# Gate of the RWKV/Fourier mixer: ScalarE copies the product out of PSUM, then one tanh and one VectorE product

## The chip, the cores and the metric

One core of one Trainium2 chip runs the whole program in one launch. The metric is the device time in microseconds (us). The engines that this text names are PE (TensorE, the matrix products), DVE (VectorE), ACT (ScalarE), POOL (GpSimd) and SP (SyncE, which issues most DMAs). Each engine works off its own row of instructions; semaphores between the engines make an instruction wait until its operands are there and its destination is free.

## The reference, cut to what matters

Two blocks follow each other, each with two layers. The change lies in the even layer of the second block, whose mixer is

```
u = h @ w_in
s, gate_r, four, gate_f = jnp.split(u, ...)
s = s + (shift_fn(s) - s) * mu          # r, k0, v and the small inner layers
... the RWKV recurrence in two directions gives o, then a norm over each head ...
yr = o * jax.nn.silu(gate_r)
yf = fourier_mix(four) * jax.nn.silu(gate_f)
return jnp.concatenate([yr, yf], axis=-1) @ w_out
```

`silu(g)` is `g * sigmoid(g)`, and the kernel forms twice that as `(tanh(g / 2) + 1) * g`; the factor of two is put into other constants. `gate_r` has six tiles of 128 channels and `gate_f` two, so there are eight such gates. A tile has 768 columns: 256 of the context (`TC`) and 512 of the grid (`T`), together `CT`.

## The kernel before

Every product of the projection is made in three matrix products of split fp32 (high times high, low times high, high times low). `project_in` computes one tile of `h @ w_in`: 24 matmuls of 256 columns into the PSUM tile `ipc` and 24 of 512 columns into the PSUM tile `ipm`. Both have one buffer each, so the next projection can't begin in `ipc` before the last reader of the previous `ipc` is done.

What reads them depends on the projection. For `v`, `r` and `k0` it is `shifted`: ACT copies both tiles into the SBUF tile `u` (one buffer), scales it into `out`, and six DVE instructions add the shifted parts from `u`. For a gate it is `project_gate`, the function that the change edits: two tanh of ACT read PSUM, and two DVE products read PSUM once more. The results of all of them (`v`, `r`, `k0`, `sg`) stand in seven rotating SBUF buffers with the tag `rkv` (`NRKV = 7`), except for one Fourier gate, which has its own place.

The channels go in six pairs of heads, p = 0 to 5. `slot(i)` for i = 0 to 11 works off the recurrence of pair i // 2 in direction i % 2 (a chain of small matmuls `ch` and DVE instructions `zd`), and prepares the next one: products `gb`, an inverse by back substitution on DVE (`un`, `tmp`), which goes out and back through DRAM (`ad`, `blocks`), and `couple` (the matmuls `p`, then `pb`). Beside it runs the side work: in even slots `keys` (the norm `hst`, `hr`, `rt`, then the broadcast matmuls `hbc` and `hbm`, then `kk`) and `prepare` (`wlc`, `wl`, `alm`, then `sig`, `kd`, three scans into `L`, then `DC`, `F` and `L` on ACT); in odd slots `prepare` alone and `bonus` (`o`, `boc`, `bom`). The projections fill PE between these steps, in the order

```
for p in range(6):
    if p < 5:
        tasks += [self.project_pair(hs, P[p + 1], p + 1, n) for n in ("v", "r")]
    tasks += [self.project_gate(hs, P[p], p)]
    if p < 4:
        tasks += [self.project_pair(hs, P[p + 2], p + 2, "k0")]
```

Below, v4 is the projection of `v` for pair 4, g2 the gate of pair 2, and so on. The code gives the order of the work; a scheduler then settles the order in each engine's row by its own estimate of when each instruction could run, so that an edit in one function can move instructions of others.

Of the kernel before, what the change touches and what calls it, by code (L numbers as in the profile page):

```python
# [10 lines left out]
AF = mybir.ActivationFunctionType  # L11
ALU = mybir.AluOpType
# [5 lines left out]
TC = 256  # L18
# [130 lines left out]
class K:  # L149
# [1197 lines left out]
    def project_gate(self, hs, S, p, key="sg", **place):  # L1347

        pc, pm = yield from self.project_in(hs, 20 + p)
        sg = self.e("sg", [self.CT], **(place or dict(tag="rkv", bufs=self.NRKV)))  # L1350
        self.act(sg[:, :TC], pc, AF.Tanh, scale=0.5)
        self.act(sg[:, TC:], pm, AF.Tanh, scale=0.5)
        self.stt(sg[:, :TC], sg[:, :TC], 1.0, pc, ALU.add, ALU.mult)
        self.stt(sg[:, TC:], sg[:, TC:], 1.0, pm, ALU.add, ALU.mult)
        S[key] = sg

    def prepare(self, S, p, d):
# [679 lines left out]
```

## Time and profile before

| what | value |
|---|---|
| time, three runs | 3367.13, 3380.83 and 3379.16 us, median 3379.16 |
| the profiled execution's own time | 3377.71 us |
| its span, first to last instruction | 3376.0 us |
| mean granted clock of PE | 0.962 of full speed |
| PE busy | 3165.4 us (94% of the span) |
| DVE busy | 1834.4 us (54%) |
| ACT busy | 1189.2 us (35%) |
| slots 0 to 11 with what stands between them | about 2200 to 2960 us of the span |

The shares are means over the whole program. The part in which the gates stand is less than a quarter of the span. Times below are counted from the span's start.

### The profile page before, as it was taken

What the parts mean: (1) busy time and instruction counts of PE and PEld (TensorE: products, weight loads), DVE (VectorE), ACT (ScalarE), POOL (GpSimd) and SP (SyncE); (2) the same over time, 40 slices, a digit from 0 to 9 for tenths busy, and PEclk for the clock granted to TensorE, in tenths of its full rate; (3) what the DMA queues carried; (4) which work ended last, traced back from release to release, by engine and by line L of the source; (5) the groups of instructions that cost most, each with busy time, mean ns of one, the idle gap of its engine ahead of it and who ended that gap; (6) DMA issues with size and microseconds to landing.
All of it is one profiled execution on the core that took longest, in us unless ns stands there. A gap on an engine that the chain in (4) does not pass through costs nothing. (4 is left out here: it accounts for less than half of the span.)

```text
span 3376.0 us, 58396 instructions
## 1 busy us (share of the span) xinstructions
PE 3165.4 (94%) x24530; PEld 2646.8 (78%) x24530; DVE 1834.4 (54%) x3336; ACT 1189.2 (35%) x1925; POOL 287.1 (9%) x285
## 2 busy tenths in 40 slices
PE   5999999999999999999999979999898899869998
PEld 4877887888889888878887868788787778758766
DVE  8554378444425554364667456456655655462554
ACT  4222244432223222344322234233332432242553
POOL 3000020200002000111000010011101111020000
PEclk8999999999999999999999989999999999979999
DMA  6555421144433554332355521211110111222112
GB/s 238 191 181 178 134 82 44 51 145 143 131 96 120 185 176 164 121 102 78 117 182 182 163 87 46 72 31 38 32 30 22 29 58 30 59 67 63 62 39 69
DMA packets 156503, 340.90 MB, mean 101 GB/s; under 512 B 52816, under 2 KB 64848, under 8 KB 156112
## 3 DMA queue, kind: packets, MB, share of 16 engines
q1 hardware_dynamic: 156240, 337.18, 30.8%
q8 instruction: 192, 3.15, 0.4%
q14 instruction: 71, 0.58, 0.1%
HBM read 328.20 MB, written 8.91 MB: 100 GB/s over the span
## 5 line engine op out<-in xcount | busy, mean ns | idle before, releaser
L169 ACT ACTIVATE whi<-raw 128x1024 fp32r<-128x1024 f32 (+2 forms) x451 | 426.0, 947 | 1122.1 <-PE po L174 266.4
L253 DVE TENSOR_TENSOR wlo<-raw,whi 128x1024 fp32r<-128x1024 f32 (+2 forms) x432 | 471.3, 1093 | 539.7 <-ACT whi L169 528.8
L313 DVE CUSTOM_DVE_ANT_0 raw_a<-raw_a,cond 128x1024 f32<-128x1024 f32 x176 | 215.4, 1230 | 339.2 <-DMA raw_a<-in_ada_w_dram 339.1
L174 PE MATMUL pu<-hh,whi 128*128 128x512 f32 (+1 forms) x824 | 317.5, 385 | 5.0 <-ACT whi L169 5.0
L174 PE MATMUL pu<-hh,wlo 128*128 128x512 f32 (+1 forms) x824 | 316.5, 384 | 2.9 <-DVE wlo L253 2.9
L174 PE MATMUL pu<-hl,whi 128*128 128x512 f32 (+1 forms) x824 | 316.2, 384 | 0.0
L174 PE MATMUL pg<-hh,whi 128*128 128x512 f32 (+1 forms) x752 | 293.6, 391 | 22.1 <-ACT hh L169 20.0
L174 PE MATMUL po<-ah,whi 128*128 128x512 f32 (+1 forms) x880 | 309.7, 352 | 3.0 <-ACT sq L169 3.0
L174 PE MATMUL po<-ah,wlo 128*128 128x512 f32 (+1 forms) x880 | 308.7, 351 | 0.0
L174 PE MATMUL po<-al,whi 128*128 128x512 f32 (+1 forms) x880 | 308.0, 350 | 0.0
L174 PE MATMUL pg<-hl,whi 128*128 128x512 f32 (+1 forms) x752 | 291.9, 389 | 5.2 <-DVE hl L188 5.2
L174 PE MATMUL pg<-hh,wlo 128*128 128x512 f32 (+1 forms) x752 | 292.3, 389 | 4.4 <-DVE wlo L253 4.2
L402 POOL TENSOR_TENSOR x<-x,y 128x256 f32<-128x256 f32 x106 | 77.2, 763 | 2107.7 <-DVE y L188 2107.4
L174 PEld LDWEIGHTS pg<-hh,whi 128*128 128x128 f32 x752 | 147.1, 196 | 53.7 <-ACT hh L169 22.2
L174 PEld LDWEIGHTS pu<-hh,whi 128*128 128x128 f32 x824 | 159.0, 193 | 37.4 <-ACT whi L169 5.8
L174 PEld LDWEIGHTS po<-ah,whi 128*128 128x128 f32 x880 | 166.2, 189 | 27.5 <-ACT sq L169 3.8
L174 PEld LDWEIGHTS pu<-hh,wlo 128*128 128x128 f32 x824 | 158.2, 192 | 36.1 <-DVE wlo L253 4.5
L174 PEld LDWEIGHTS po<-al,whi 128*128 128x128 f32 x880 | 166.2, 189 | 23.5
L174 PEld LDWEIGHTS po<-ah,wlo 128*128 128x128 f32 x880 | 166.2, 189 | 23.3
L174 PEld LDWEIGHTS pu<-hl,whi 128*128 128x128 f32 x824 | 158.6, 193 | 31.9
L174 PEld LDWEIGHTS pg<-hh,wlo 128*128 128x128 f32 x752 | 146.3, 195 | 37.5 <-DVE wlo L253 8.4
L174 PEld LDWEIGHTS pg<-hl,whi 128*128 128x128 f32 x752 | 146.0, 194 | 36.0 <-DVE hl L188 6.7
(468 smaller groups left out, 6507.5 us busy)
## 6 DMA issues: line engine op xcount, KB each, us to landing
raw<-in_w_dram SPq DMA_DIRECT2D x232, 512.0 KB, 4.1
raw_a<-in_ada_w_dram SPq DMA_DIRECT2D x176, 512.0 KB, 3.7
raw<-in_ev_in_dram SPq DMA_DIRECT2D x60, 256.0 KB, 2.6
raw<-in_w_dram SPq DMA_DIRECT2D x32, 384.0 KB, 3.6
raw_a<-in_ada_w_dram SPq DMA_DIRECT2D x32, 256.0 KB, 5.6
raw<-in_ab_in_dram SPq DMA_DIRECT2D x16, 512.0 KB, 3.2
raw<-in_ev_out_dram SPq DMA_DIRECT2D x20, 256.0 KB, 2.7
raw<-in_w_dram SPq DMA_DIRECT2D x16, 256.0 KB, 2.6
```

The source lines that it names most:

```text
L169: ins = self.nc.scalar.activation(out=out, in_=in_, func=func, scale=scale, bias=bias)
L174: self.last_mm = self.nc.tensor.matmul(out, lhsT=lhsT, rhs=rhs, start=start, stop=stop)
L253: (self.nc.gpsimd if self.nwt <= self.POOLW else self.nc.vector).tensor_tensor(out=lo, in0=src, in1=hi.bitcast(F32), op=ALU.subtract)
L313: self.nc.vector.tensor_tensor_reduce(out=out, in0=raw, in1=v, scale=1.0, scalar=0.0, op0=ALU.mult, op1=ALU.add, accum_out=dst[:, o : o + 1])
L402: done = (self.nc.vector if last and k % 2 == 0 and (c0 or k > 4) else self.nc.gpsimd).tensor_tensor(out=new, in0=new, in1=y[k - 1][:, col ...
```

## The change

`project_gate` gets a tile `u`, which is the buffer that `shifted` uses too (same name, same shape, one buffer). ACT copies `ipc` and `ipm` into it; one tanh of 768 columns and one DVE product of 768 columns read the copy.

```
         pc, pm = yield from self.project_in(hs, 20 + p)
         sg = self.e("sg", [self.CT], **(place or dict(tag="rkv", bufs=self.NRKV)))
-        self.act(sg[:, :TC], pc, AF.Tanh, scale=0.5)
-        self.act(sg[:, TC:], pm, AF.Tanh, scale=0.5)
-        self.stt(sg[:, :TC], sg[:, :TC], 1.0, pc, ALU.add, ALU.mult)
-        self.stt(sg[:, TC:], sg[:, TC:], 1.0, pm, ALU.add, ALU.mult)
+        u = self.e("u", [self.CT])
+        self.act(u[:, :TC], pc, AF.Copy)
+        self.act(u[:, TC:], pm, AF.Copy)
+        self.act(sg, u, AF.Tanh, scale=0.5)
+        self.stt(sg, sg, 1.0, u, ALU.add, ALU.mult)
         S[key] = sg
```

The rows of the engines change in more places than these. ACT's row in slot 4, from the second tanh of `sig` on (`hr` is the inverse norm, `rt` its copy for the broadcast, `u` the copied projection, `whi` the high part of a weight), before:

```order
L169 ACTIVATE kd<-alm,a0h 128x512
L169 ACTIVATE whi<-raw 128x512
L169 ACTIVATE u<-ipm 128x512
L169 ACT_TABLE_LOAD
L169 ACTIVATE hr<-hst 128x12
L169 ACT_TABLE_LOAD
L169 ACTIVATE DC<-L 128x12
L169 ACTIVATE F<-L 128x12x64
L169 ACTIVATE r<-u,omu 128x768
L169 ACTIVATE rt<-hr 128x768
L169 ACTIVATE L<-L 128x768
```

and after:

```order
L169 ACTIVATE kd<-alm,a0h 128x512
L169 ACTIVATE whi<-raw 128x512
L169 ACTIVATE DC<-L 128x12
L169 ACTIVATE F<-L 128x12x64
L169 ACT_TABLE_LOAD
L169 ACTIVATE hr<-hst 128x12
L169 ACT_TABLE_LOAD
L169 ACTIVATE L<-L 128x768
L169 ACTIVATE rt<-hr 128x768
L169 ACTIVATE u<-ipc 128x256
L169 ACTIVATE whi<-raw 128x512
L169 ACTIVATE u<-ipm 128x512
```

`DC` and `F`, which read the scans, now stand ahead of `hr` and `rt`, and the copies of g3 stand behind `rt`; the projection r4, whose copies stood here, has moved to the slot before. In slot 2 the row has the same turn, and there it is the copy `u<-ipm` of v3 that stands behind `DC`, `F`, `hr` and `L`. Slot 6 is as slot 4.

PE's row in slot 4, around the broadcast `hbc` and `hbm` of the norm and the first matmuls `p` of `couple` (`ipc` and `ipm` are a projection's two PSUM tiles), before:

```order
L174 MATMUL hbc<-cst,rt 128x128 x2
L174 MATMUL hbm<-cst,rt 128x128 x4
L174 MATMUL ipm<-ehh_14770,wlo 128x512
L174 MATMUL ipm<-ehh_14772,whi 128x512
L174 MATMUL ipm<-ehl_14773,whi 128x512
L174 MATMUL ipm<-ehh_14772,wlo 128x512
L174 MATMUL ipm<-ehh_14774,whi 128x512
L174 MATMUL ipm<-ehl_14775,whi 128x512
L174 MATMUL ipm<-ehh_14774,wlo 128x512
L174 MATMUL p_20410<-tn,am_20402 64x64 x16
```

and after:

```order
L174 MATMUL ipm<-ehl_14775,whi 128x512
L174 MATMUL ipm<-ehh_14774,wlo 128x512
L174 MATMUL hbc<-cst,rt 128x128 x2
L174 MATMUL hbm<-cst,rt 128x128 x4
L174 MATMUL ipc<-ehh_14760,whi 128x256
L174 MATMUL ipc<-ehl_14761,whi 128x256
L174 MATMUL ipc<-ehh_14760,wlo 128x256
L174 MATMUL ipc<-ehh_14762,whi 128x256
L174 MATMUL ipc<-ehl_14763,whi 128x256
L174 MATMUL ipc<-ehh_14762,wlo 128x256
```

Before, the rest of g3 (7 matmuls) stands between the broadcast and `p`. Now g3 is complete ahead of the broadcast, and k5 begins behind it: 22 matmuls of 256 and 12 of 512 columns stand ahead of `p`, and the other 2 and 12 behind its first group.

ACT's row in slot 3, around the gate g2, before:

```order
L169 ACTIVATE DC<-L 128x12
L169 ACTIVATE F<-L 128x12x64
L169 ACTIVATE kd<-kd,oka,kah 128x768
L169 ACTIVATE L<-L 128x768
L169 ACTIVATE sg<-ipc 128x256
L169 ACTIVATE sg<-ipm 128x512
L169 ACTIVATE whi<-raw 128x512
L169 ACTIVATE u<-ipc 128x256
```

and after:

```order
L169 ACTIVATE DC<-L 128x12
L169 ACTIVATE F<-L 128x12x64
L169 ACTIVATE kd<-kd,oka,kah 128x768
L169 ACTIVATE L<-L 128x768
L169 ACTIVATE whi<-raw 128x512
L169 ACTIVATE sg<-u 128x768
L169 ACTIVATE u<-ipc 128x256
L169 ACTIVATE u<-ipm 128x512
```

The tanh of g2 keeps its place; its copies have gone to slot 2, and right behind it stand the copies of k4 into the same buffer `u`. On DVE the product `sg<-sg,u` stands where the two products stood, behind `kd<-kd,k`, `kk` and `o<-kd`. In slot 4 and in slot 6 DVE's three scans `L<-ec,sig`, which stood within the back substitution, now stand behind all of it but its last step, and the six instructions of r4 (r5 in slot 6), which stood behind it, within it. In slot 7, PE's row has no projection left ahead of `p`: the matmuls `eoc` and `eom` of the output projection stand there instead.

## Rows read from the trace of the kernel before

**Rows 1.** What PE waited for, 2200 to 2960 us: total, times, longest.

```profile
PE ipc L174 <- DVE sg L188: 32.2, 4, 10.4
...
PE p L174 <- DVE tn L1538: 4.3, 2, 2.2
```

**Rows 2.** PE in slot 3: start, duration, instruction, idle time before and its releaser.

```profile
2419.10 0.59 PE L174 MATMUL alm<-al,a2t 64*128 64x512 f32 x1
2430.11 0.58 PE L174 MATMUL ipc<-ehh,whi 128*128 128x256 f32 x1 [10.42 <-DVE sg L188]
2430.48 0.41 PE L174 MATMUL ipc<-ehl,whi 128*128 128x256 f32 x1
2430.70 0.42 PE L174 MATMUL ipc<-ehh,wlo 128*128 128x256 f32 x1
```

**Rows 3.** ACT in slot 3.

```profile
2428.36 0.38 ACT L169 ACTIVATE sg<-ipc 128x256 f32<-128x256 f32 x1 [0.44 <-DVE kd L183]
```

**Rows 4.** DVE in slot 3.

```profile
2427.38 0.95 DVE L183 TENSOR_TENSOR kd<-kd,k 128x768 f32<-128x768 f32 x1
```

**Rows 5.** All instructions with tile sg: shortest, median, longest in ns.

```profile
L169 ACT ACTIVATE sg<-ipc x8: 383/383/386, 2117.5 to 2711.1; 128x256 f32<-128x256 f32 x8
L188 DVE SCALAR_TENSOR_TENSOR sg<-sg,ipc x8: 405/410/423, 2117.9 to 2711.5; 128x256 f32<-128x256 f32 x8
L169 ACT ACTIVATE sg<-ipm x8: 574/586/592, 2122.0 to 2711.9; 128x512 f32<-128x512 f32 x8
L188 DVE SCALAR_TENSOR_TENSOR sg<-sg,ipm x8: 675/678/684, 2123.2 to 2712.7; 128x512 f32<-128x512 f32 x8
L188 DVE SCALAR_TENSOR_TENSOR o<-o,lb,sg x6: 1018/1019/1019, 2357.7 to 2944.5; 128x768 f32<-128x768 f32 x6
```

**Rows 6.** ACT in slot 2.

```profile
2365.97 0.58 ACT L169 ACTIVATE u<-ipm 128x512 f32<-128x512 f32 x1
2366.57 1.28 ACT L169 ACT_TABLE_LOAD   x1
...
2369.49 0.83 ACT L169 ACTIVATE F<-L 128x768 f32<-128x768 f32 x1
...
2372.52 0.62 ACT L169 ACTIVATE whi<-raw 128x512 fp32r<-128x512 f32 x1
```

**Rows 7.** DVE in slot 2.

```profile
2365.07 1.86 DVE L1388 TENSOR_TENSOR_SCAN L<-ec,sig 128x256 f32<-128x256 f32 x3 [0.59 <-ACT sig L169]
```

**Rows 8.** PE in slot 2.

```profile
2366.64 0.28 PE L174 MATMUL ipc<-ehh,whi 128*128 128x256 f32 x1
2366.76 0.28 PE L174 MATMUL ipc<-ehl,whi 128*128 128x256 f32 x1
2366.89 0.40 PE L174 MATMUL ipm<-ehh,whi 128*128 128x512 f32 x1
2367.12 0.40 PE L174 MATMUL ipm<-ehl,whi 128*128 128x512 f32 x1
```

**Rows 9.** DVE in slot 4.

```profile
2506.11 0.17 DVE L183 TENSOR_TENSOR un<-un,tmp 96x26 f32<-96x26 f32 x1
...
2509.66 2.78 DVE L188 SCALAR_TENSOR_TENSOR r<-u,mug,r 128x504 f32<-128x504 f32 x5 [2.64 <-ACT r L169]
```

**Rows 10.** PE in slot 4.

```profile
2510.45 0.67 PE L174 MATMUL hbc<-cst,rt 128*128 128x128 f32 x4
...
2515.80 1.67 PE L174 MATMUL p<-tn,am 64*64 64x64 f32 x48 [2.16 <-DVE tn L1538]
2518.42 3.00 PE L174 MATMUL p<-g,blocks 64*64 64x64 f32 x48 [0.95 <-ACT g L169]
```

**Rows 11.** DVE in slot 7.

```profile
2702.71 1.04 DVE L1538 STREAM_TRANSPOSE tn<-blocks 128x512 f32<-128x512 f32 x2 [3.22 <-DMA blocks<-ad]
```

**Rows 12.** PE in slot 7.

```profile
2705.47 1.61 PE L174 MATMUL p<-tn,am 64*64 64x64 f32 x48
...
2719.74 0.33 PE L174 MATMUL pb<-gb,tn 64*64 64x64 f32 x4 [0.33 <-DVE tn L183]
```

## The prediction

> **What bounds the kernel now.** I read the list of what PE waited for first, because PE is busy 94% of the span and a change elsewhere counts only through it. Between 2200 and 2960 us one entry is far above the rest: the first matmul of a projection (`ipc`) waits 32.2 us in four waits for a DVE instruction on `sg`, the longest 10.4 [rows 1]. So a gate's late reading of PSUM does stop PE. The timeline of PE shows where: in slot 3, `alm` is issued at 2419.10 and the next matmul only at 2430.11, after 10.42 us [rows 2]. Slots 5 and 7 repeat it.
>
> Why is the gate late there? ACT's row has the tanh of `sg` at 2428.36, released by `kd` of DVE [rows 3]: the tanh writes an `rkv` buffer, and the last reader of its former content is `kd<-kd,k`, at 2427.38 for 0.95 us [rows 4]. The gate therefore waits for a slot in SBUF, and holds its two PSUM tiles meanwhile. A copy into another tile doesn't need that slot. That is the good side of the change. The cost of the stall goes beyond the idle time: behind it 256-column matmuls start 0.22 us apart (2430.48 to 2430.70 [rows 2]) and in an undisturbed stretch 0.12 (2366.64 to 2366.76 [rows 8]), the lower of the two clock levels against the higher. About 20 matmuls run so, some 20 x 0.10 = 2.0 us.
>
> **The edit by itself.** For one gate ACT loses tanh of 0.38 and 0.59 us and gets two copies of the same shapes and source, taken as equal, and a tanh of 768 columns, 0.83 by the nearest row, `F<-L` [rows 5, 6]: 8 x 0.83 = 6.6 us more on an engine that is busy 35%. DVE loses 0.41 + 0.68 = 1.09 and gets one product of 768 columns, no dearer than `o<-o,lb,sg` at 1.02 and taken as 0.95 like `kd<-kd,k` [rows 5, 4]: 8 x 0.14 = 1.1 us less. Either sum is hidden where PE has work queued, and counts in full only where a wait hangs on it: from -1.1 to +6.6 us.
>
> The Trainium skill, "VectorE: DVE Perf Modes", Rules for kernel authors, advises to copy out of PSUM first only where many operations follow. Here one follows, and the rows agree that little is saved on DVE (0.14 us a gate); by that rule alone the sum would be the 6.6 us of ACT at worst.
>
> **What moves.** The order of the rows decides more than these sums, slot by slot. Two things matter: `u` is one buffer shared with `shifted`, and ACT's row is worked off in order.
>
> *Slot 2.* Before, ACT copies `ipm` of v3 at 2365.97 for 0.58 us, and r3 writes `ipm` at 2366.89 without a wait [rows 6, 8]. Now the copy stands behind `DC`, `F`, `hr` with two table loads, `L` and `whi`. The scans end at 2365.07 + 1.86 = 2366.93 [rows 7]; then 0.2 + 0.83 + 1.28 + 0.2 + 1.28 + 0.83 + 0.62 + 0.58 (durations of rows 6, the small ones and `L` as `F`) gives 2372.7, so 5.8 us of new idle time on PE. The 2.9 us of k4 that this slot takes over (12 x 0.12 + 7 x 0.23 less what slack there is) partly fill waits of `couple`. From +5.8 to +9; I take +7.
>
> *Slot 3.* v4 can't begin before k4 has been copied to `u`, and that copy waits for the gate's product. The first DVE product ended as PE was released, at 2430.1. In its place stands one of 0.95, then a copy of 0.38: 2430.1 - 0.41 + 0.95 + 0.38 = 2431.0 [rows 2, 4, 5]. So the wait stays, ending 0.9 later; k4's 16 matmuls (3.2 us) now run before it, and 23 instead of 37 stand behind it. I take -0.8, between +0.9 and -2.4.
>
> *Slot 4.* Before, `hbc` starts at 2510.45 and `p` at 2515.80, after 2.16 us of idle time [rows 10]. Now six `shifted` instructions (2.78 for five [rows 9]) stand in the back substitution and the scans behind it; the two swaps about cancel, so the last but one step of `un` ends near 2506.2 [rows 9]. Then scans 1.86, `DC` and `F` 1.0, load, `hr`, load 2.8, `L` and `rt` 1.65 (as in slot 2): `hbc` at 2513.5. g3 has been used up by then and k5 needs `ipc`, copied behind `rt`; PE idles some 5 us. Behind `hbc` (1.4 us with `hbm`) 22 x 0.12 + 12 x 0.23 = 5.4 us of k5 stand before `p`: 2520.3, so +4.5 at the higher clock. The 14 matmuls behind the first group of `p` (3.0 us) cover its 0.95 us wait: +2.0. If the clock has fallen, up to 34 x 0.10 = 3.4 more: I take 1. Sum +7.5, from +4 (the cover is better) to +10.
>
> *Slot 5.* About 4.4 us of work (12 matmuls of 256, 13 of 512 columns) have gone to slot 4. The wait of 10.4 us stays and ends 0.9 later, as in slot 3; what is missing stood between the groups of `couple`, where waits for ACT and DVE remain. Between 0 and -4.4, I take -1.7.
>
> *Slot 6.* As slot 4, with g4 and g5, and with the split of the Fourier part (`eyl`) in DVE's row ahead of `up`. +9, from +5 to +11.
>
> *Slot 7.* No projection is left to wait for PSUM. `p` can start when the blocks are back, 2702.71 + 1.04 = 2703.75, or at 2702.7 with its first half, against 2705.47 [rows 11, 12]: -2.5. From `p` to `pb` it took 14.25 us [rows 12]; without the last 11 matmuls of g5 (2.5 us) -2.5. Sum -5.
>
> *Slot 10* has a few matmuls between other groups: +1, between 0 and +2. The other slots keep their order up to a few rows: 0. The extra time on ACT is within these terms.
>
> **Sum.** 7 - 0.8 + 7.5 - 1.7 + 9 - 5 + 1 = +17.0 us on 3377.7 (span 3376.0 and 1.7 around it): 3394.7. The median of the runs is 1.5 higher than the profiled execution: 3396. Adding all lower bounds and all upper bounds gives +3 and +33; single terms being independent, I take 3384 to 3411 for this case.
>
> **Rivals.**
> *A, the stalls go.* The copies free PSUM early, as the code reads, and the three waits of 10.4 us vanish with their slow matmuls: 3 x (10.4 + 2.0) = 37 us, 3341. For it: four waits of PE on `sg` carry 32.2 us [rows 1]. Against: `p` can't come earlier than the blocks (in slot 7, 2.8 us [rows 11, 12]), so more likely 10 to 25 us: 3353 to 3368. It decides if the copies of g2 and g3 let k4 and k5 finish before the stall and nothing new is late in slots 2, 4 and 6, as where the scans come early enough to hide the turn of ACT's row.
>
> The Trainium skill, "Perfetto Trace Analysis", Optimization Strategy, reads gaps that repeat as too few buffers for the next tile; by that rule freeing PSUM early would take these three away, 37 us. The trace agrees that a buffer is what is missing, but of SBUF, and `u` would be the next one.
>
> *B, nothing on balance.* The stall moves from PSUM to `u`, and the turned rows of slots 2, 4 and 6 find slack: new waits of about 2 us each instead of 5, as `p` waited for the blocks anyway (4.3 us in two waits [rows 1]). 3 x 2 - 5 = +1: 3370 to 3384.
>
> *C, worse.* The clock falls behind each new wait and stays low for a whole `couple` (some 10 us of PE at half speed, 5 us each): 3396 + 3 x 5 = 3411 and more.
>
> **How the numbers follow.** Forecast 0.60 (0.38 of it above 3396), B 0.22, A 0.14, C 0.04. No change within 0.5%, about what a measurement of this kernel can tell, is 3362 to 3396: 0.22 and 0.22 less the part of A that lies there, some 0.44 in all; slower 0.38 + 0.04 = 0.42; faster 0.14. The range reaches from 3360, which cuts most of A, to 3412, which cuts C.
>
> **What would show it.** Right: in slots 2, 4 and 6 PE has new waits of 5 to 7 us ended by ACT (`u` or `rt`); in slots 3 and 5 a wait of 8 and 11 us remains, ended by ACT `u` and no longer by DVE `sg`; in slot 7 `p` starts about 2.5 us sooner after the blocks' issue. Each step is wrong if these rows are absent: if `u` ends no long wait in slots 3 and 5, A holds; if `p` in slots 4 and 6 still waits for `tn`, the inverse and not the broadcast is last there, and B holds. What would upset the sum most is the scans: if they come earlier than reckoned, the terms of slots 2, 4 and 6 (+23.5) shrink together.

## The result and the profile after

| | before | after |
|---|---|---|
| median of five runs of each, one chip | 3379.08 us | 3396.86 us |
| lowest to highest | 3367.13 to 3380.83 | 3395.53 to 3404.26 |
| ratio after / before, 95% interval | | 1.0066 [1.0048, 1.0084] |
| profiled execution, its span | 3377.7, 3376.0 | 3404.26, 3402.5 |

The change costs 17.8 us by the medians. The profiled execution of after is the slowest of its five, 7.4 us above their median, so what follows, read from it, adds up to more than that. First the page of after, span and busy times:

```profile
span 3402.5 us, 58400 instructions
...
PE 3178.3 (93%) x24530; PEld 2648.1 (78%) x24530; DVE 1834.8 (54%) x3328; ACT 1198.1 (35%) x1933; POOL 293.8 (9%) x285
```

The spans differ by 26.5 us, and nothing on this page says why: the same matmuls, and DVE and ACT as far from full as before. What PE waited for between 2200 and 2990 us (total, times, longest) is the view that answers to [rows 1]; it reaches 30 us further, since the slots end later. One more entry of before stands below it:

```profile
PE ipc L174 <- ACT u L169: 23.1, 4, 11.4
PE hbc L174 <- ACT rt L169: 14.8, 5, 4.8
PE eoc L174 <- ACT u L169: 11.4, 1, 11.4
PE eoc L174 <- ACT eyh L169: 5.3, 2, 4.3
PE ipc L174 <- ACT whi L169: 4.4, 1, 4.4
PE p L174 <- DVE tn L1539: 3.1, 1, 3.1
```

```profile
PE hbc L174 <- ACT rt L169: 5.7, 3, 2.9
```

The reader is to see two things. The long waits on the gate haven't gone, they have changed hands: `sg` of DVE ended 32.2 us of them [rows 1], and `u` of ACT now ends 23.1 + 11.4 us. And there are new ones: one on `whi`, and two long ones on `rt`, which ended three short waits before. Both are instructions of ACT.

The span can be laid out by slots. Each `couple` has one first `pb` on PE; a slot is here the stretch from the first `pb` of the couple before it to its own. The starts (us), from PE's timeline of each kernel, the first being that of the main couple ahead of slot 0, the second that of slot 0:

```
before 2179.67 2250.89 2322.33 2391.99 2459.02 2526.09 2592.63 2659.68 2719.74 2791.11 2852.09 2911.51
after  2182.76 2256.53 2327.84 2405.56 2475.53 2548.93 2612.81 2688.28 2741.40 2812.20 2874.05 2937.43
```

Slot 2, say, took 2391.99 - 2322.33 = 69.66 us and takes 2405.56 - 2327.84 = 77.72. In the same way for all slots, and for the experiments below, each against before (us, one profiled execution each):

| kernel | ahead of slot 0 | 0 | 1 | 2 | 3 | 4 | 5 | 6 | 7 | 8 | 9 | 10 | slots 0 to 10 |
|---|---|---|---|---|---|---|---|---|---|---|---|---|---|
| after | 3.1 | 2.6 | -0.1 | 8.1 | 2.9 | 6.3 | -2.7 | 8.4 | -6.9 | -0.6 | 0.9 | 4.0 | +22.8 |
| old_order | 0.2 | 2.7 | 0.0 | 0.0 | -2.5 | -0.7 | -1.0 | -0.9 | -1.8 | -1.5 | 0.8 | 0.0 | -4.9 |
| turned_back | 6.8 | 1.2 | -0.2 | 7.6 | 3.1 | 1.8 | -2.1 | 5.3 | -6.8 | -1.1 | 1.2 | 4.1 | +14.2 |
| turned_back2 | -2.5 | 1.2 | -0.2 | 2.9 | 3.7 | 1.6 | -1.6 | 5.0 | -6.4 | -1.5 | 0.0 | 2.3 | +6.9 |
| own_u | -1.1 | -0.7 | -1.7 | 8.1 | 1.0 | 7.3 | -3.5 | 7.3 | -7.1 | -0.8 | 0.9 | 3.9 | +14.7 |
| early_copies | 0.0 | 2.4 | -1.6 | 0.0 | -1.3 | -0.8 | -0.4 | -0.6 | 0.0 | -1.4 | 0.3 | 0.0 | -3.4 |
| double_tanh | 6.7 | 4.8 | 0.0 | 0.0 | -2.6 | -0.9 | -2.5 | -0.9 | -1.1 | -0.6 | 0.8 | 0.4 | -2.5 |
| old_own_u | -0.8 | 0.0 | -1.5 | 0.0 | -1.6 | -0.8 | -2.1 | -0.9 | -2.2 | -0.3 | 1.4 | 0.0 | -7.9 |
| filled | 5.3 | 2.4 | -1.6 | 0.0 | -2.0 | -0.9 | -2.2 | -0.9 | -4.6 | -1.1 | 0.8 | 0.0 | -10.0 |
| best | 6.5 | 0.0 | -1.5 | 0.0 | -5.6 | -0.9 | -6.7 | -0.8 | -2.6 | -2.3 | 0.7 | 0.0 | -19.7 |

The column ahead of slot 0 (from -2.5 to +6.8 us) is nearly all there when ACT first reads a gate (at 2117.49 us in before, 2120.55 in after), so it is what one execution differs by from another, and not the edit. A slot whose rows are the same repeats far better: slot 2 gives 0.0 in six kernels, slot 7 -6.9 to -6.4 in the three that have after's rows there; slot 0 is the loosest, with 1.2 to 2.6 in the same three. Slots are therefore compared with slots, and medians with medians.

The four large terms of after, each in its rows. Slot 2, PE and then ACT (start, duration, instruction, idle time before and its releaser):

```profile
2378.21 0.58 PE L174 MATMUL ipc<-ehh,whi 128*128 128x256 f32 x1 [4.37 <-ACT whi L169]
```

```profile
2373.04 0.22 ACT L169 ACTIVATE DC<-L 128x12 f32<-128x12 f32 x1 [2.83 <-DVE L L1389]
...
2376.80 0.84 ACT L169 ACTIVATE L<-L 128x768 f32<-128x768 f32 x1
2377.55 0.61 ACT L169 ACTIVATE whi<-raw 128x512 fp32r<-128x512 f32 x1
2378.07 0.58 ACT L169 ACTIVATE u<-ipm 128x512 f32<-128x512 f32 x1
```

`whi`, the split of r3's weights, stands in ACT's row behind everything that hangs on DVE's scans; it starts at 2377.55, ends at about 2378.16, and PE goes on at 2378.21. The copy that the prediction blamed comes after it. Slots 4 and 6, the broadcasts; slots 3, 5 and 7, the gates; slot 10, all on PE:

```profile
2450.76 0.58 PE L174 MATMUL ipc<-ehh,whi 128*128 128x256 f32 x1 [8.27 <-ACT u L169]
...
2529.85 1.12 PE L174 MATMUL hbc<-cst,rt 128*128 128x128 f32 x4 [4.50 <-ACT rt L169]
...
2538.34 1.61 PE L174 MATMUL p<-tn,am 64*64 64x64 f32 x48
...
2587.98 0.58 PE L174 MATMUL ipc<-ehh,whi 128*128 128x256 f32 x1 [11.36 <-ACT u L169]
...
2667.27 1.22 PE L174 MATMUL hbc<-cst,rt 128*128 128x128 f32 x4 [4.78 <-ACT rt L169]
...
2727.34 0.58 PE L174 MATMUL eoc<-eyh,whi 128*128 128x256 f32 x1 [11.36 <-ACT u L169]
2732.50 1.61 PE L174 MATMUL p<-tn,am 64*64 64x64 f32 x48
...
2922.86 2.83 PE L174 MATMUL p<-tn,am 64*64 64x64 f32 x48 [3.09 <-DVE tn L1539]
```

The waits of 10.4 us [rows 2] are here as 8.27, 11.36 and 11.36 us, ended by ACT `u`. The broadcasts have got new ones of 4.50 and 4.78. Behind them `p` starts without a wait, where it waited 2.16 us for `tn` [rows 10]: the blocks are no longer the last to come. In slot 7 the first matmul of the output projection waits 11.36 us, a microsecond more than g5's did before, and the slot is still 6.9 us shorter, mostly since no matmuls of g5 are left between `p` and `pb`.

### The profile page after: what moved, and what is told of

It is laid out like the page before. It is cut to its first block, busy times and chain, and to the rows that moved or that the text cites. A ratio compares the mean times of both kernels' runs of the same rounds, so it can differ in the third digit from the quotient of the medians.

```text
span 3402.5 us, 58400 instructions
## 1 busy us (share of the span) xinstructions
PE 3178.3 (93%) x24530; PEld 2648.1 (78%) x24530; DVE 1834.8 (54%) x3328; ACT 1198.1 (35%) x1933; POOL 293.8 (9%) x285
```

## The experiments

In all kernels below the order of the rows is given by hand between 2080 and 2960 us: a table holds for PE, ACT, DVE and SP the wanted sequence, and each instruction gets an edge to the one ahead of it that fixes the order of issue and nothing else. No run holds the order of before or of after unedited; but slot 2 in the old order comes out as in before to 0.01 us, and slot 7 in turned_back and turned_back2 as in after to 0.5.

```
for a, b in zip(at, at[1:]):
    tc.add_manual_dep(row[b], row[a].name, info, reason="order")
```

**1. The edit without its order (old_order).** The gate as in the change; every row in the order of before, with the copies and the tanh where the two tanh stood.

```diff
-ACT: DC F kd L  sg<-ipc sg<-ipm       whi u<-ipc
+ACT: DC F kd L  u<-ipc u<-ipm sg<-u   whi u<-ipc
```

> The whole edit, but each engine's row held in the order of the kernel before: the two copies and the tanh of a gate stand where its two tanh stood, the one product where the second product stood. Theory (the loss comes from the rows that the scheduler turned, not from the edited instructions): no loss; the copies start behind L on ACT in slots 3, 5 and 7 without waiting for kd of DVE, so PE is released some 1.7 us earlier there; 3 x 1.7 = 5 us less at best, nothing at worst: 3374 to 3380, ratio to before 0.998 to 1.000, and the new waits of PE in slots 2, 4 and 6 (whi, rt) are gone. Rival 1 (the 6.6 us of added work on ACT are paid): 3383 to 3388. Rival 2 (the shared buffer u is what costs): the waits of 8 to 11 us ended by u in slots 3, 5, 7 remain beside the others, 3390 to 3397.

Measured: 3371.69 us against 3377.57, ratio 0.9983 [0.9973, 0.9993], somewhat better than expected. The edit by itself is worth some 6 us (2 to 9 by the interval); the order that came with it cost 25 by the medians (3396.86 - 3371.69), 28 by the slots (22.8 + 4.9). Slot 3 shows the good side, PE first, then DVE:

```profile
2431.19 0.58 PE L174 MATMUL ipc<-ehh,whi 128*128 128x256 f32 x1 [8.55 <-ACT u L169]
...
2438.89 1.61 PE L174 MATMUL p<-tn,am 64*64 64x64 f32 x48
```

```profile
2437.51 1.04 DVE L1539 STREAM_TRANSPOSE tn<-blocks 128x512 f32<-128x512 f32 x2 [2.56 <-DMA blocks<-ad]
```

A copy ends the wait in place of a tanh, that had to wait for `kd`, and a product: 8.55 for 10.42 us [rows 2], and the slot is 2.5 us shorter. Slot 2 changes by 0.0, slots 4 and 6 by -0.7 and -0.9: the whole of after's +8.1, +6.3 and +8.4 belongs to the rows' order. Slot 0 is 2.7 us longer. There g0's copies write `u`, and PE waits for it:

```profile
2233.22 0.39 PE L174 MATMUL ipc<-ehh,whi 128*128 128x256 f32 x1 [2.30 <-ACT u L169]
```

**2. The turned rows turned back (turned_back, turned_back2).** After's order, but what PE waits for stands ahead of what hangs on the scans. The second kernel moves the weight splits of slot 2 as well.

```diff
 slot 2
-ACT: kd DC F hr L whi u<-ipm rt v          (after)
+ACT: kd hr u<-ipm rt DC F L whi v          (turned_back)
+ACT: whi hr u<-ipm rt DC F L v             (turned_back2; wlo likewise on DVE)
 slots 4, 6
-ACT: whi DC F hr L rt u<-ipc whi u<-ipm
+ACT: whi hr rt u<-ipc DC F L whi u<-ipm
 slots 2, 4, 6
+DVE: hr ahead of the scans
```

> The changed kernel with its own rows held, but in slots 2, 4 and 6 the turn on ACT is undone: hr and rt (slot 2: hr, the copy u<-ipm of v3 and rt; slots 4 and 6: hr, rt and the copy u<-ipc of the gate) stand ahead of DC, F and L, and on DVE the two small hr instructions ahead of the three scans. Theory: PE's waits of 4.4, 4.5 and 4.8 us in these slots shrink below 1 us, p comes 4 to 6 us earlier in each, 13 to 16 us in all: 3381 to 3384, ratio to before 1.0005 to 1.0015; the waits ended by u in slots 3, 5 and 7 stay at 8 to 11 us. Rival 1 (the work on ACT or the shared buffer costs): no change, 3395 to 3399. Rival 2 (p is late for its blocks, not for hbc): less than 4 us in all, 3393 to 3397.

> As turned_back, and in slot 2 the weight split (whi on ACT, wlo on DVE) stands ahead of hr too. In turned_back PE still waited 3.7 us there, for whi and not for the copy of v3. Theory (slot 2 is lost to the weight split behind DC, F, hr and L, not to the copy u<-ipm that the prediction named): that wait goes, slot 2 costs 2 to 4 us instead of 7.6, and the time falls by 4 to 5 us against turned_back: 3387 to 3389, ratio to before 1.003 to 1.004. Rival (the copy or the blocks are last there): the wait only changes its releaser, less than 1.5 us gained.

Measured: 3392.71 us, ratio 1.0049 [1.0037, 1.0062], and 3389.07, ratio 1.0036 [1.0022, 1.0049]. The first missed its expectation: 13 to 16 us were to come, and 4 came by the medians, 8.6 by the slots. The second fell by 3.6 us more for 4 to 5, which is within the runs' spread, with slot 2 as expected. In turned_back slot 4 falls from +6.3 to +1.8 and slot 6 from +8.4 to +5.3, but slot 2 stays at +7.6. Its rows say why, ACT and then PE in slot 2:

```profile
2374.78 0.60 ACT L169 ACTIVATE u<-ipm 128x512 f32<-128x512 f32 x1 [0.75 <-PE ipm L174]
...
2379.20 0.61 ACT L169 ACTIVATE whi<-raw 128x512 fp32r<-128x512 f32 x1
```

```profile
2379.87 0.58 PE L174 MATMUL ipc<-ehh,whi 128*128 128x256 f32 x1 [3.69 <-ACT whi L169]
```

The copy into `u` runs 4 us before PE is released and does nothing for it. With `whi` and `wlo` ahead as well slot 2 falls to +2.9. So some 5 us of slot 2 come from ACT's turned row, and the instruction is the weight split. The 2.9 us that stay stand behind `p`: in turned_back2 `p` starts 2.4 us sooner in the slot than in before, and from `p` to `pb` it takes 19.9 us for 14.7, with 71 projection matmuls there for 36. In slot 4 the next one in line shows, on PE:

```profile
2527.21 0.61 PE L174 MATMUL hbc<-cst,rt 128*128 128x128 f32 x4
...
2535.89 1.61 PE L174 MATMUL p<-tn,am 64*64 64x64 f32 x48 [1.48 <-DVE tn L1539]
```

`hbc` no longer waits, and `p` now waits 1.48 us for the blocks, so here the expectation's second rival holds in part. Of the 4.50 us, 4.5 come back in this slot (6.3 - 1.8), in slot 6 3.1 of 4.78. There `p` starts 0.7 us sooner in the slot than in before, but from `p` to `pb` it takes 16.3 us for 10.3, with a new wait in the middle:

```profile
2678.33 2.35 PE L174 MATMUL p<-tn,am 64*64 64x64 f32 x48 [3.43 <-DVE tn L183]
```

Against after the slots 2, 4 and 6 together gain 8.0 us and then another 5.3 (their sums, 22.8, 14.8 and 9.5); no run takes away what stays of them.

**3. The gate's own buffer (own_u, old_own_u).** The gate's copy gets a tile of its own; `us` gives up one of its buffers for the room. own_u has after's order and copies k4 and k5 ahead of the scans' results; old_own_u is old_order with that tile.

```diff
-u = self.e("u", [self.CT])
+u = self.e("ug", [self.CT])
-us = self.e("us", [4, 64], bufs=5)
+us = self.e("us", [4, 64], bufs=4)
 own_u, slots 3, 5
+ACT: u<-ipc u<-ipm of k4, k5 ahead of DC
```

> The changed kernel with its own rows held, the gate's copy in a buffer of its own (the tile us gets 4 buffers instead of 5 to make room) and, in slots 3 and 5, the next projection's two copies into u ahead of DC on ACT. Theory (in slots 3 and 5 the single u keeps the next projection waiting for the gate's product): PE's waits of 8.3 and 11.4 us there end at 1 to 3 us; p gains only its slack against the blocks, 3.2 and 2.3 us by the changed kernel's trace: 4 to 6 us in all, 3391 to 3393, ratio to before 1.004 to 1.005. Rival 1 (u is not what holds it, but PSUM or a weight): the waits stay, 3396 to 3398. Rival 2 (the waits are paid in full): 17 us, 3380.

> The edit in the order of the kernel before (old_order), with the gate's copy in a buffer of its own (us with 4 buffers instead of 5). Nothing else moves. In old_order, slot 0 is 2.7 us longer than before: the copy of g0 waits until the instructions of an earlier projection have read u, and PE waits 2.3 us for it where it waited 0.9. Theory (that is the price of the shared buffer, paid in slot 0 alone as long as the order is the old one): slot 0 loses no time, 2.5 to 3 us less than old_order by the slots of the trace, no change in slots 3, 5 and 7, where ACT's row puts the copies behind L anyway: 3367 to 3371. Rival (slot 0 differs by chance between executions): slot 0 stays 2 to 3 us longer than before.

Measured: own_u 3392.57 us, ratio 1.0044 [1.0031, 1.0058]; old_own_u 3370.06, ratio 0.9977 [0.9968, 0.9987]. PE in slot 3 of own_u:

```profile
2437.28 0.38 PE L174 MATMUL ipc<-ehh,whi 128*128 128x256 f32 x1 [2.27 <-ACT whi L169]
...
2440.65 0.58 PE L174 MATMUL ipc<-ehh,wlo 128*128 128x256 f32 x1 [2.86 <-DVE wlo L253]
...
2444.17 2.45 PE L174 MATMUL p<-tn,am 64*64 64x64 f32 x48 [0.59 <-DVE tn L1539]
```

The wait of 8.27 us on `u` is gone, and in its place stand 2.27 for `whi`, 2.86 for `wlo` and 0.59 for the blocks; `p` runs in 2.45 us instead of 1.61. The slot gains 1.9 us (+2.9 to +1.0). Slot 5 gains 0.8: the wait of 11.36 us falls to 2.37, and 6.72 us appear in front of `p`. The time came out as expected, but not from where it was expected: 4 to 6 us were reckoned for slots 3 and 5, which gave 2.7; slots 0 and 1 gave some 3 and 1.6, and slots 4 and 6 lost and gained one. In old_own_u slot 0 goes from +2.7 to 0.0, as in best and, to -0.7, in own_u: the shared buffer was the cause there. By the medians old_own_u and old_order can't be told apart (3370.06 and 3371.69). The wait of slot 3 stays at 8.55 us, now ended by `ug`, since the copy stands behind `DC`, `F`, `kd` and `L` as before.

**4. The stall taken away (early_copies).** Old order, but the copies of g2, g3 and g4 go ahead of the scans' results on ACT, so that PSUM is free early. This is rival A made true.

```diff
 slots 3, 5, 7
-ACT: kd DC F kd L u<-ipc u<-ipm sg<-u
+ACT: kd u<-ipc u<-ipm DC F kd L sg<-u
```

> As the edit in the order of the kernel before, with one move: in slots 3, 5 and 7 the gate's two copies stand ahead of DC, F, kd and L on ACT, where ACT waited 3.5 us for the scans. Theory: PE's three waits of 10.4 us for sg end at 2 to 3 us, the next projection's first 37 matmuls run early, and p is then late only for its blocks: 4 us each in slots 3 and 5, 2.7 in slot 7, with less of the low clock: 10 to 14 us, 3365 to 3370, ratio 0.996 to 0.997. Rival 1 (nothing is gained, as u and not PSUM holds the next projection): 3376 to 3380. Rival 2 (all three waits go with their slow matmuls): 3341 to 3350.

Measured: 3380.77 us, ratio 1.001 [1.0, 1.0019]: the expectation failed. The waits did go, as this view of PE, 2200 to 2960 us, shows:

```profile
PE p L174 <- DVE tn L1539: 22.9, 5, 7.1
...
PE ipc L174 <- ACT u L169: 11.1, 6, 2.4
```

In old_order these two entries are 4.5 us (longest 2.4) and 29.8 us (longest 8.6). So 18.7 us of waiting on the gate were removed and 18.4 appeared on `tn`. Slot 3, PE and DVE:

```profile
2422.93 0.56 PE L174 MATMUL ipc<-ehh,whi 128*128 128x256 f32 x1 [2.37 <-ACT u L169]
...
2436.30 2.83 PE L174 MATMUL p<-tn,am 64*64 64x64 f32 x48 [5.76 <-DVE tn L1539]
```

```profile
2435.44 1.04 DVE L1539 STREAM_TRANSPOSE tn<-blocks 128x512 f32<-128x512 f32 x2 [3.04 <-DMA blocks<-ad]
```

The wait is 6.2 us shorter (8.55 less 2.37), the matmuls behind it are done sooner, and PE then stands 5.76 us before `p`, which needs blocks that come back by DMA. Most of the stall was time that PE would have waited anyway. And `p`, after the idle time, takes 2.83 us and not 1.61. Against before, `p` starts 3.0, 2.7 and 2.5 us sooner in slots 3, 5 and 7, and from `p` to `pb` it takes 1.7, 2.4 and 2.6 us longer, so that the slots gain 1.3, 0.4 and 0.0. One thing stays open: the median is 9.1 us above that of old_order, while the slots differ by 1.5. The profiled execution is the fastest of the eleven, 7.8 us below their median, and doesn't show what the others spent.

**5. The price of the tanh (double_tanh).** old_order with the tanh issued twice, to see whether 0.85 us more on ACT for each gate is felt.

```diff
 self.act(sg, u, AF.Tanh, scale=0.5)
+self.act(sg, u, AF.Tanh, scale=0.5)
```

> As the edit in the order of the kernel before, with each gate's tanh of 768 columns issued twice (the second writes the same values): 8 x 0.83 = 6.6 us more on ACT once again. Theory: the added work of ACT is hidden except where DVE's product of the gate waits for it, which releases nothing on PE at once: 0 to 2 us more than the edit in the old order. Rival 1 (ACT's work is paid in full): 6 to 7 us more.

Measured: 3376.96 us, ratio 1.0 [0.9991, 1.0008]. Against old_order that is 5.3 us by the medians (the runs' spread leaves some 1.5 to 8) and 2.4 us by the slots, 2.1 of them in slot 0. The 0 to 2 us expected are missed by the medians, and the rival, that the added 8 x 0.85 = 6.8 us are paid in full, is not excluded. The trace shows only that slots 2 to 6, with the stalls of slots 3 and 5 among them, are no longer than in old_order.

**6. The idle time filled (filled).** early_copies, and PE gets work ahead of the first `p`: 23 matmuls of the next projection in slots 3 and 5, 11 in slot 7, which stood behind it.

```diff
 slots 3, 5
-PE: ipc ipm ipc ipm | p  (23 of them behind p)
+PE: ipc 20 ipm 12 ipc 4 ipm 1 | ipm 11 ipc 12 | p boc bom p
```

> As early_copies, and on PE 23 matmuls of the next projections (slots 3 and 5: 11 of k, 12 of v; slot 7: 11 of g5) stand ahead of the first group of p instead of behind it. In early_copies PE idles 5.8 us before p, which waits for its blocks, and the work behind p makes couple long. Theory (with the copies early, the path of slots 3, 5 and 7 runs through the blocks and the projections left in couple): the idle time before p shrinks to 2 to 3 us, couple is 2.5 to 4 us shorter in each slot, 8 to 11 us less than early_copies, within the slots as the trace shows them, and less than the edit in the old order by 5 to 9: 3363 to 3370, ratio to before 0.995 to 0.998. Rival (couple is bound by its chain over ACT and DVE): the slots keep their length, 3371 to 3380.

Measured: 3370.12 us, ratio 0.9973 [0.9963, 0.9983], 10.7 us less than early_copies, as expected. Against old_order, where 5 to 9 us were expected, it is 1.6 us less by the medians, with intervals that overlap, and 5.1 by the slots, 2.8 of them in slot 7 (slot 3 is 0.5 longer). PE, 2200 to 2960 us:

```profile
PE ipc L174 <- DVE wlo L253: 8.8, 3, 4.5
PE p L174 <- DVE tn L1539: 7.3, 3, 3.0
```

The wait on the blocks falls from 22.9 to 7.3 us. What is late next is `wlo`, the low half of the split, on DVE behind the gate's product and the wait for the blocks.

**7. All of it (best).** filled with the gate's own buffer, and in slots 3 and 5 the splits ahead of the gate's arithmetic.

```diff
-ACT: kd u<-ipc u<-ipm DC F kd L sg<-u whi u<-ipc
+ACT: kd ug<-ipc ug<-ipm DC F kd L whi u<-ipc sg<-ug
-DVE: sg<-sg,u sq tn wlo
+DVE: wlo sg<-sg,ug sq tn
```

> As filled, with the gate's own buffer, and in slots 3 and 5 the weight split of the next projection ahead of the gate's tanh (ACT) and product (DVE), with the first copy of k behind it, since filled showed PE waiting 3.8 us there for wlo. Theory: in slots 3 and 5 p starts as soon as its blocks are there, 1.5 to 2.5 us earlier than in filled, and slot 0 gains 2.5 to 3 us: 5 to 8 us less than filled: 3362 to 3366, ratio to before 0.994 to 0.9965. Rival (p was late for its blocks in filled anyway, and slot 0 differs by chance): 3368 to 3371.

Measured: 3364.21 us against 3378.1 for before, ratio 0.9964 [0.995, 0.9978], span 3361.4. It beats both kernels, before by some 14 us and after by 33. What PE still waits for, and its `p` in slot 3:

```profile
PE p L174 <- DVE tn L1539: 9.3, 4, 4.5
PE ipc L174 <- ACT ug L169: 7.1, 3, 2.4
...
PE p L174 <- POOL ka L1469: 4.9, 2, 3.4
```

```profile
2440.53 2.83 PE L174 MATMUL p<-tn,am 64*64 64x64 f32 x48 [3.42 <-POOL ka L1469]
```

```profile
2439.67 1.04 DVE L1539 STREAM_TRANSPOSE tn<-blocks 128x512 f32<-128x512 f32 x2 [2.52 <-DMA blocks<-ad]
```

The last two fences are PE and DVE in the same stretch: the first of the two transposes is done half-way, about 2440.19, and `p` starts at 2440.53, 0.34 later, as in early_copies (2435.44 + 0.52 = 2435.96, `p` at 2436.30). From the transposes' start to `p` it is 0.86 us in both, and 0.84 to 0.86 wherever `p` waits for the transposes in these traces. By time, then, it is still `tn` that `p` waits for, although the profile names `ka`. Against old_own_u, which differs from best by the early copies, the filling and the order of the splits and has the same runs of before beside it, best is 5.9 us faster by the medians and 11.8 by the slots.

## Why the prediction was right

Forecast 3396 us, measured 3396.86. The level was right, and partly by luck: the profiled execution of after stands 26.5 us above that of before by span and the medians 17.8, against the sum's +17.0, and by slots the terms miss by -1.9 to +3.7 us:

| slot | forecast | after | what the runs showed |
|---|---|---|---|
| 2 | +7 | +8.1 | ACT's turned row; PE waits for `whi`, not for `u` (experiment 2) |
| 3 | -0.8 | +2.9 | the wait is there, 8.27 us for the 8 named, but ends 7.1 us later in the slot, not 0.9 |
| 4 | +7.5 | +6.3 | wait for `rt`, 4.50 of some 5 us; gone when turned back |
| 5 | -1.7 | -2.7 | wait for `u`, 11.36 us for the 11 named; the gain stands from `p` to `pb`, 18.0 us for 20.6 |
| 6 | +9 | +8.4 | as slot 4, 4.78 us |
| 7 | -5 | -6.9 | less work between `p` and `pb`; a wait for PSUM remained |
| 10 | +1 | +4.0 | matmuls that stood ahead of `p` stand behind it: `p` waits 3.09 us for `tn` and then takes 2.83 us |
| 0, 1, 8, 9 | 0 | +2.7 | slot 0: g0's copies wait for the shared `u` |
| sum | +17.0 | +22.8 | |

Of the signs that it named, those of slots 3 and 5 came as written. The new waits in slots 2, 4 and 6 are 4.4, 4.5 and 4.8 us for the 5 to 7 named, and the first is ended by `whi`, not by `u` or `rt`. In slot 7 `p` starts 1.6 us sooner in the slot for 2.5.

**The edit by itself.** Forecast from -1.1 to +6.6 us, and hidden. The instructions came out as priced, tile `sg` of after (shortest, median, longest in ns):

```profile
L169 ACT ACTIVATE sg<-u x8: 827/844/846, 2127.7 to 2736.4; 128x768 f32<-128x768 f32 x8
L188 DVE SCALAR_TENSOR_TENSOR sg<-sg,u x8: 945/958/1484, 2128.6 to 2737.3; 128x768 f32<-128x768 f32 x8
```

That is 0.84 and 0.96 us for 0.83 and 0.95 taken. ACT's busy time rose by 8.9 us (1189.2 to 1198.1) for 6.6, DVE's by 0.4, where 1.1 less were reckoned. In the old order the edit gave 5.9 us, more than the range allowed, because there it shortens the stall itself (slots 3, 5 and 7 gain 2.5, 1.0 and 1.8 us), which the prediction named as the good side and gave no number in its sum. The Trainium skill's advice ("VectorE: DVE Perf Modes", Rules for kernel authors) to copy out of PSUM first where many operations follow is not what decided here: old_order makes the copies for one tanh and one product, and is faster than before.

**Slot 2.** The mechanism was right (ACT's row, with the scans, `DC`, `F`, `hr` and `L` ahead), the instruction wrong. The prediction let `u<-ipm` release PE at the end of its chain; `whi`, one place ahead of it in the same chain, did. The wait is 4.37 us, where 5.8 of idle time were reckoned; against that stands a term that slot 2 lacked, the low clock behind the wait, by the windows further below an estimated 2.5 us (half of 2.8 us and a fifth of 5.3). The two differences partly cancel in the time; and a cure built on the prediction's words failed: turned_back moved the copy and gained 0.4 us.

**Slots 4 and 6.** Right in the place, the releaser and the size of the wait; turned_back removes 4.5 and 3.1 us of them. The rest of slot 4's sum came out otherwise. `hbc` starts 2.9 us later in the slot for the 3.0 reckoned; from `hbc` to `p` it took 8.5 us for 6.8, and from `p` to `pb` 10.6 for 10.3 before, where +2.0 had been reckoned.

**Slots 3 and 5.** That the stall stays and changes its releaser from `sg` to `u` was right to 0.4 us. The size of slot 3 was off by 3.7 us, outside the -2.4 to +0.9 given. The term that failed is the end of the wait, put 0.9 us later: it came 45.20 us after the slot's start for 38.12, 7.1 later. That the wait has the length named is luck, since it also begins 9.2 us later and not 3.2. The shorter rest behind it did arrive (5.1 us from the wait to `p` for 8.35). Before and then after, PE and DVE in slot 3:

```profile
2393.91 1.04 PE L174 MATMUL pq<-bt,a0T 64*64 64x128 f32 x16
2423.22 0.68 DVE L1388 TENSOR_TENSOR_SCAN L<-ec,sig 128x256 f32<-128x256 f32 x1
```

```profile
2409.61 1.09 PE L174 MATMUL pq<-bt,a0T 64*64 64x128 f32 x16
2440.53 1.84 DVE L1389 TENSOR_TENSOR_SCAN L<-ec,sig 128x256 f32<-128x256 f32 x3
2447.68 1.21 DVE L253 TENSOR_TENSOR wlo<-raw,whi 128x512 fp32r<-128x512 f32 x1
2448.82 1.48 DVE L188 SCALAR_TENSOR_TENSOR sg<-sg,u 128x768 f32<-128x768 f32 x1
```

Nine projection matmuls now stand between `pb` and the first `pq`, which starts 2.1 us later in the slot; the scans have turned behind the back substitution here too and start 3.7 us later; and between them and the gate's product stands `wlo`, the product itself taking 1.48 us. In own_u, which takes the wait away, the first two are the same and the slot is still +1.0. No run turns these rows back one by one, so the split of the 7.1 us among them is read, not shown.

**Slot 7.** "No projection is left to wait for PSUM" was wrong. `eoc` uses the same PSUM tiles and waits 11.36 us. It costs little, because `p` can't come ahead of the blocks anyway; DVE of after:

```profile
2730.49 1.04 DVE L1539 STREAM_TRANSPOSE tn<-blocks 128x512 f32<-128x512 f32 x2 [2.69 <-DMA blocks<-ad]
```

`p` starts 2.01 us behind these transposes, where 0.84 is the least in these traces, so 1.2 us at most. The slot gained more than reckoned, -6.9 for -5. From `p` to `pb` it took 2741.40 - 2732.50 = 8.90 us for 14.27 (2719.74 - 2705.47 [rows 12]; the prediction has 14.25), 5.4 less where 2.5 was reckoned; the start of `p` gave the other 1.6, for 2.5. There the prediction misread a row: 2702.7 is where the transposes start, and the first half is done at 2702.71 + 0.52 = 2703.2.

**Slots 0 and 10** were put too low. In slot 0 the shared `u` costs 2.6 us, shown by old_own_u; the prediction named the sharing and priced it only in slots 3 and 5. As for its range, the upper bounds that it gives add up to +28 with slot 7 at -5; +33 takes slot 7 as nothing, which it doesn't say.

**Rival A** didn't hold in after, and early_copies shows that in the old order it wouldn't have been worth 37 us, nor 10 to 25: with the waits on PSUM down to 2.4 us the median is no better than before. `p` comes earlier only as far as the blocks allow, 2.5 to 3.0 us, and most of that is lost again behind it. The prediction had the blocks as the argument against A, and took it too lightly. The rule of the Trainium skill, "Perfetto Trace Analysis", Optimization Strategy, that a repeated gap can mean too few buffers, is borne out for the gap (8.6 us in old_order, 2.4 once copied early) and not for the time. **Rival B** is refuted by slots 2, 4 and 6, +22.8 us together where it had 3 x 2. **Rival C** isn't seen. The clock does fall behind the long waits, but comes back within the same slot, as the windows of after show in slot 2, behind the wait of 4.37 us (span; its length; busy time of PE, PEld, DVE, ACT and POOL; granted clock; DMA):

```profile
2378.20:2381.00 2.80, 2.79 (x8) 2.31 (x8) 2.40 (x5) 2.00 (x3) 0.00 (x0) 0.50 0.28 93
2381.00:2386.30 5.30, 5.30 (x29) 4.57 (x27) 3.44 (x7) 0.63 (x1) 0.00 (x0) 0.79 0.04 12
2386.30:2388.00 1.70, 1.70 (x51) 1.58 (x49) 1.67 (x4) 0.45 (x1) 0.00 (x0) 1.00 0.33 118
```

Right behind the wait the clock is 0.50, the lower level (1.2 GHz), and at `p` it is 1.00, the upper one (2.4). In slots 4 and 7 of after, too, `p` takes its 1.61 us, with projection matmuls between the wait and `p`.

## What to carry to other kernels

When an order is planned from the code, a small edit can move rows far away from it: read what moved on each engine first, and time the edit in the old order too; here the one was worth 6 us and the other cost 25 to 28. Before a stall is attacked, look at what the work behind it waits for next: freeing PSUM alone brought nothing, with matmuls to fill the gap it drew level with the old order (1.6 us ahead by the medians, not clear of noise), and only with the splits moved as well and a buffer of its own was it 6 to 7.5 us ahead (3364.21 against 3370.06 and 3371.69). Of a row that has turned, the first instruction in it that PE needs is the one that stalls it, and a cure has to move that one.

## What the hardware showed beside this

The first `p` group, 48 matmuls of 64 columns, takes from 1.61 to 2.83 us, and the granted clock of the stretch goes with it. The clock is 1.00 from 2438.80 to 2440.50 in old_order, and 0.50 from 2436.20 to 2439.10 in early_copies, behind 5.76 us of idle time; 0.50 too in slot 10 of after (3.09 us idle). In filled it was 0.50 as well, although ten matmuls (2.37 us of work) stood between the idle 3.77 us and `p`. So an idle stretch just before a `couple` can cost 1.2 us more than itself, and I had reckoned the loss only for the wide matmuls behind a gate. It doesn't always: in slot 7 of filled `p` follows 2.98 us of idle time and takes 1.61 us, at 1.00 from 2703.00 to 2704.70.

An execution also starts the slots up to 9.3 us later than another with the same rows ahead of them (turned_back against turned_back2), so a few us can't be read from two traces without laying them out in stretches.
